# Ten products with the identity, in float32, issued as transposes of TensorE

## The chip, the cores and the metric

The kernel runs on one core of a Trainium2 chip. The metric is the device time of one execution in microseconds (us). The core's engines work side by side, each in an order of its own: TensorE (PE in the profile, with PEld for its weight loads), VectorE (DVE), ScalarE (ACT), GpSimd (POOL) and SyncE (SP), which issues most transfers. A matmul has a stationary operand, which a weight load puts into the array, and a moving operand, whose columns stream through it; the result goes to PSUM.

## The reference

One sequence of 512 tokens with 1024 features, in float32, goes through two blocks of two layers each. Cut to what matters:

```python
def first_block(x, c, ...):
    cond = silu(c)
    for l in range(2):
        sh1, sc1, g1, sh2, sc2, g2, sh3, sc3, g3 = split(cond @ w_ada[l] + b_ada[l], 9)
        x = x + 0.5 * g1 * swiglu(modulate(rms_norm(x), sh1, sc1), w_ff1_in[l], w_ff1_out[l])
        z_a, z_b, z_c = split_cols(modulate(rms_norm(x), sh2, sc2) @ w_in[l], ...)
        o = concat([rwkv7_mixer(z_a, ...), mla_mixer(z_b, ...), retention_mixer(z_c, ...)])
        x = x + g2 * (o @ w_out[l])
        x = x + 0.5 * g3 * swiglu(modulate(rms_norm(x), sh3, sc3), w_ff2_in[l], w_ff2_out[l])
    return rms_norm(x) * final_norm_g

def second_block(x, ...):
    h = x
    for l in range(2):
        p_in, dq, dk, dv, gq, gk, gv, gr, gg = split(rms_norm(h, norm1_g[l]) @ w_in[l])
        mix = concat([pool_mixer(p_in), diff_attention(dq, dk, dv), gla_mixer(gq, gk, gv, gr, gg)])
        h = h + mix @ w_out[l]
        h = h + square(relu(rms_norm(h, norm2_g[l]) @ w_mlp1[l])) @ w_mlp2[l]
    return rms_norm(h, final_norm_g)

reference = second_block(first_block(x, c, ...), ...)
```

The `rwkv7_mixer` is a linear recurrence in both directions with four heads of 64; `mla_mixer` is attention with eight heads over latent keys and values; `retention_mixer` is a decayed linear attention; `diff_attention` takes the difference of two softmax maps for each of four heads; `gla_mixer` is a gated linear attention in chunks of 64 tokens.

## The kernel before

Activations lie with the features on the 128 partitions and the 512 tokens along the free axis, in eight chunks. Wide products (`gemm`) are made of two float32r parts for each operand: three matmuls of 128x128 weights by 512 columns stand for one float32 product. The weights come by DMA as float32 and are split into the two parts by ScalarE (a cast) and VectorE (a subtraction). The program is, for each layer of the first block, a feed-forward part (`ff`), a mixer (`mixer1`) and another `ff`, then for each layer of the second block a mixer (`mixer2`) and an `mlp`. In time: the first mixers lie at about 400 to 870 and 1600 to 2100 us, the second mixers at about 2430 to 2650 and 3030 to 3250 us; the rest is wide products.

In a mixer two streams are merged. `merge` issues one stream (in `mixer1` the recurrence of `rwkv`, in `mixer2` the three mixers by turns) and fills each of its pauses with a hand-set amount of the other (the projections of the tokens, the attention, the retention). The pauses are the numbers after `yield`. The instructions so written pass through the framework's scheduler, which makes each engine's order from priorities and modelled durations and puts in the semaphores. The order on an engine is thus near the program's, but not the same everywhere.

Some steps need data turned from features on partitions to tokens on partitions, or a value of each token on all partitions. The kernel does both with a plain float32 matmul that has the data as the stationary operand and the identity (`self.ident`, 128x128) as the moving one, 128 columns at a time, four column blocks to a PSUM bank:

- `bcast` (line 503): the norm's factor of each token, one column for 128 tokens, read with a step of zero as a 128x128 stationary. It serves the norms of both blocks and the two latent norms (`mla_norms`).
- `head_bcast` (line 740): the same for factors of a head, spread to 64 columns by VectorE first.
- `rwkv_pair` (lines 985 and 996): six blocks for each pair of chunks, for each pair of heads; ScalarE copies the result out.
- `rwkv_heads` (line 1101), `mla_pair` (line 1234): outputs turned back to features on partitions.
- `diff` (lines 1651 and 1671): the difference of the softmax maps, t + 1 blocks for token tile t of a head, then the head's output.
- `gla` (lines 1709 and 1778): the keys, and the output.

An engine's calls go through a helper (`Spy.call`, line 136) that notes which tiles they name, so nearly all rows of the profile bear line 136, and the tiles tell them apart. Another product, in `mla_first`, uses `ident_r`, the identity as float32r, with a stationary of one column; the change doesn't touch it. `rms_col` makes the sum over the features with a moving operand of one column of ones.

Of the kernel before, what the change touches and what calls it, by code (L numbers as in the profile page):

```python
# [20 lines left out]
P = 128  # L21
# [26 lines left out]
# ---------------------------------------------------------------- host layout  # L48
def blocks(w, cols=P):
    """[K, N] -> [N/cols, 128, K/128*cols]: one contiguous run per partition and block."""  # L50
    k, n = w.shape
    return np.ascontiguousarray(
        w.reshape(k // P, P, n // cols, cols).transpose(2, 1, 0, 3)
    ).reshape(n // cols, P, (k // P) * cols)


def group_blocks(w, groups):
    """[K, N] -> per group of K chunks: [N/128, 128, kg*128], flattened and joined."""
    return np.concatenate([blocks(w[a * P:(a + n) * P]).ravel() for a, n in groups])
# [15 lines left out]
def make_masks():  # L75
    """constants that depend on shapes alone."""
# [23 lines left out]
def make_rows():  # L100
    """rotary frequencies and the sign of the sine, per partition, for head widths 64 and 32."""
    out = np.zeros((P, 4), np.float32)
    base = np.float32(10000.0)
    for j, d in ((0, 64), (2, 32)):
        inv = base ** (-np.arange(0, d, 2, dtype=np.float32) / np.float32(d))
        out[:, j] = np.tile(inv, P // (d // 2))
        out[:, j + 1] = np.where(np.arange(P) % d < d // 2, -1.0, 1.0)
    return out
# [11 lines left out]
# ---------------------------------------------------------------- device side  # L120
# [4 lines left out]
class Spy:  # L125
    """an engine that notes which tiles each instruction names, then issues it."""
# [21 lines left out]
class Alloc:  # L148
    """Tiles by class. A dry pass notes where each is used first and last in program order; from that each gets
    one of the class's fixed buffers, so that the buffers never force an order that the program doesn't have."""  # L150
# [17 lines left out]
    def begin(self, cls, key, n):  # L168
        """buffers (key, 0..n-1) that serve the class until `end`."""
# [5 lines left out]
    def assign(self, sizes):  # L175
        """key of the buffer for every tile, in the order of their birth."""
# [6 lines left out]
    def assign_with(self, sizes, keep):  # L183
        """the same, with `keep` buffers of a class held back from what fits into one that comes and goes."""
# [25 lines left out]
# class of buffer -> (shape, type, count); the phase's own classes follow  # L210
# [15 lines left out]
# places of the first mixer that change their use: the stages' classes; "x" lies where "h" of the phase "ff" does  # L226
# [7 lines left out]
class Build:  # L234
# [36 lines left out]
    def stage(self, i):  # L271
        """the places from the first that changes on pass over to the classes of stage i."""
# [31 lines left out]
    def lend_x(self):  # L304
        """put x into DRAM; until it is back its tiles serve as the phase's slots."""
# [49 lines left out]
    def background(self, share=None):  # L355
        """part of the work that goes on behind the first block's wide products (share None: all that is left)."""
# [23 lines left out]
    # -- weights: one block, split exactly into two float32r parts  # L380
    def weight(self, ap, n, cls="wr", sub=None):
        """(hi, lo) tiles of 512 columns each."""
# [17 lines left out]
    def gemm(self, out, w, x, ks, m=P, at=0, sl=ALL):  # L400
        """out[m, 512] = sum_k w_k^T x_k, each product of split parts; w's chunks from column `at` on."""
# [3 lines left out]
    def gemm_k(self, out, w, xk, i, n, m=P, at=0, sl=ALL):  # L405
        """chunk i of n of such a product."""
# [7 lines left out]
    def out_proj(self, load, g, update, norm=None, scale=None):  # L414
        """x[j] from its products with g, for all j. norm "sum": with the sums of squares of the next norm, the last
        j's left to `pending`; "halves": with the norm itself, the last two j by halves of the tokens, so that the first half's is there early."""
# [33 lines left out]
    # -- rsqrt of a small positive tile by DVE  # L450
# [14 lines left out]
    def sum_sq(self, acc, xc, sl=ALL):  # L465
        """acc + xc^2 (acc None: a new sum)."""
# [10 lines left out]
    def x_done(self, j, sl=ALL):  # L477
        """chunk j of x has its final value of this stage: its part of the next norm."""
        self.xsq = self.sum_sq(None if j == 0 else self.xsq, self.x[j], sl)

    def norm_half(self, i):
        """PSUM [128, 512], half i of the tokens: one over the norm of x."""
# [3 lines left out]
    def rms_col(self, chunks, dim, eps, ts=range(4)):  # L486
        """[128, 4]: 1/sqrt(mean over features of x^2 + eps) of token ts[t]*128 + partition; chunks None: of x."""
# [15 lines left out]
    def bcast(self, r, ts=range(4)):  # L503
        """PSUM [128, 512] with the token's value on every partition."""
        pr = self.aux_ps()
        for i, t in enumerate(ts):
            self.nc.tensor.matmul(pr[:, t * P:(t + 1) * P], r[:, i:i + 1].to_broadcast([P, P]), self.ident,
                                  start=True, stop=True)
# [5 lines left out]
    # -- adaptive layer norm: one section of 1024 columns  # L514
    def cond_row(self):
        """silu(c) on every partition."""
# [13 lines left out]
    def ada_dot(self, l, s, k, w):  # L530
        """chunk k of section s of 1024 columns of the modulation of layer l, less its bias."""
# [3 lines left out]
    def ada_end(self, l, s, k=0, n=KD):  # L535
        """chunks k.. of section s with their bias, and what is derived from them."""
# [10 lines left out]
    def ada_steps(self, parts):  # L547
        """the sections (layer, section) one after the other in small steps, loads ahead of them."""
# [13 lines left out]
    def modulate(self, i, k, hk, pr, sl=ALL, pool=True):  # L562
        """chunk k of h = rms_norm(x) * (1 + sc) + sh, split into hk."""
# [13 lines left out]
    def modulated(self, i, ws):  # L577
        """h of modulation i, a list of (hi, lo), and its products with the first weights, by halves of the tokens
        and as the chunks come."""
# [11 lines left out]
    def start(self):  # L591
        """the first h: its modulation is worked out chunk by chunk as the weights for it come in."""
# [26 lines left out]
    def ff(self, l, w, i, norm):  # L619
        """x += 0.5 * g * (silu(h w_gate) * (h w_up)) w_out"""  # L620
# [32 lines left out]
    # ------------------------------------------------------------ constants  # L653
    def restart(self):
        """factors of a scan over the tokens that starts anew with every chunk of 64."""
# [9 lines left out]
    def rotary_tables(self):  # L665
        """cos and signed sin of positions * inv, [128, 512] each, for head widths 64 and 32."""
# [26 lines left out]
    def derived(self, l):  # L693
        """small per-feature vectors worked out on chip for layer l of the first block."""
# [14 lines left out]
    # ------------------------------------------------------------ first mixer: RWKV-7  # L709
# [11 lines left out]
    def rwkv_z(self, l, h, ps, dv, z):  # L721
        """nine projected tiles after the centred shift (r 0-1, k 2-3, v 4-5, gate, decay and rate inputs);
        v with the chunks of each pair swapped."""
# [16 lines left out]
    def head_bcast(self, col, stride, at):  # L740
        """PSUM [128, 512] from token-major scalars of two heads, col[tok, t*stride + at + hh]."""
# [5 lines left out]
        for t in range(4):  # L747
            self.nc.tensor.matmul(pb[:, t * P:(t + 1) * P], ex[:, t * P:(t + 1) * P], self.ident,
                                  start=True, stop=True)
        return pb  # L750

    def head_sums(self, src, dst, at):
        """dst[tok, t*2 + at + hh] = sum over the head's 64 features of src [features, tok]."""
# [4 lines left out]
    def rwkv_norm(self, l, z, j):  # L758
        """one over the norm of each head's keys, token major."""
# [19 lines left out]
    def rwkv_prep(self, l, z, dv, lora, j):  # L779
        """the four scaled operands of each direction for one pair of heads.  # L780

        pr: [d, step pair, (p | r), (par, t)]; qm: [d, step pair, par, (q | m swapped by par), t]
        """
# [57 lines left out]
    def rwkv_inverse(self, os_):  # L841
        """X^T of every chunk, X = (1 + strict part)^-1: per pair of heads and direction
        [128 (par, s)][(step pair, hh), t]."""
# [29 lines left out]
        # matrix (j, m, d, (par, half)) on its own partition, m = (step pair, hh)  # L873
# [37 lines left out]
    def rwkv_blocks(self, xt, xa, u):  # L911
        """from the inverses of the 32 x 32 diagonal blocks those of the chunks, for one pair of heads."""
        nc = self.nc
        # off-diagonal 32-blocks
# [34 lines left out]
    def rwkv_pair(self, o, vs, xt, xd, ip):  # L949
        """per-chunk matrices of one pair of chunks in each direction: what the sequential steps need.  # L950
        xd: zeros, and room for the inverses of both chunks on the diagonal."""
# [31 lines left out]
        for d in range(2):  # L983
            cp = ip if d == 0 else 3 - ip
            nc.tensor.matmul(pp[:, d * P:(d + 1) * P], o["pr"][:, d, ip, 0, :], self.ident, start=True, stop=True)
# [7 lines left out]
        for d in range(2):  # L993
            for par in range(2):
                m = d * 2 + par
                nc.tensor.matmul(pt[:, m * P:(m + 1) * P], o["qm"][:, d, ip, par].rearrange("p w t -> p (w t)"),
                                 self.ident, start=True, stop=True)
# [42 lines left out]
    def rwkv_heads(self, l, z, o, xt, gate, j, out):  # L1040
        """one pair of heads: sequential steps over the chunks, head norm, bonus, gate."""
# [5 lines left out]
        # the state by turns in two halves, both heads' [key, value] on the diagonal for each direction  # L1047
# [32 lines left out]
        # head norm (the values were centred, so the mean is zero), gain, bonus, gate  # L1080
# [19 lines left out]
        for t in range(4):  # L1100
            nc.tensor.matmul(py[:, t * P:(t + 1) * P], y[:, t * P:(t + 1) * P], self.ident, start=True, stop=True)
# [33 lines left out]
    # ------------------------------------------------------------ first mixer: latent attention  # L1135
# [19 lines left out]
    def rope32(self, out, pz, n, tab):  # L1155
        """rotary over 32-wide heads on n partitions; pz in PSUM."""
# [8 lines left out]
    def mla_norms(self, l, z):  # L1165
        """the two latent norms, in place."""
# [8 lines left out]
    def mla_first(self, z, i, pk, pq, kq, qpe):  # L1175
        """operands of head i: [64 plain, 32 rotary, 1 for the maximum] x tokens, split."""
# [9 lines left out]
        # the maximum of a row of scores, taken of the rounded operands: any number near it serves  # L1186
# [800 lines left out]
```

## Time and profile before

| | |
|---|---|
| time, median of 3 runs | 3662.97 us (3648.62 to 3664.79) |
| profiled execution: span, first to last instruction | 3653.2 us |
| PE busy | 3528.1 us (97%), 17786 matmuls |
| PEld busy | 2849.3 us (78%), 17786 loads |
| DVE busy | 2103.8 us (58%) |
| ACT busy | 1436.7 us (39%) |
| POOL busy | 281.7 us (8%) |
| mean granted clock of TensorE | 0.980 |

The profiled execution's own time is known by its span alone, 3653.2 us; it lies 9.8 us below the median and inside the range of the three runs. Busy times are shares of the span; PE's records overlap one another, since matmuls are pipelined and their ends are modelled. The granted clock is 1 at 2.4 GHz and 0.5 at 1.2 GHz.

### The profile page before, as it was taken

How to read it: one execution, taken by the hardware profiler on the slowest of the kernel's cores; microseconds unless marked ns; L12 is line 12 of the kernel's file. 1: busy time of each engine (PE TensorE's matmuls, PEld its weight loads, DVE VectorE, ACT ScalarE, POOL GpSimd, SP SyncE). 2: the span in 40 equal slices, each digit the busy share in tenths (PEclk: the TensorE clock that was granted, in tenths of full speed). 3: DMA queues.
4: the chain of work that ended last, by engine and by line, in shares of the span. 5: the costliest groups of instructions: out<-in, count | busy, mean ns of one | idle time of the engine just before them, and what ended most of it. 6: DMA issues, size and time to landing. Idle time of an engine off the chain costs nothing. (4 is left out here: it accounts for less than half of the span.)

```text
span 3653.2 us, 46456 instructions
## 1 busy us (share of the span) xinstructions
PE 3528.1 (97%) x17786; PEld 2849.3 (78%) x17786; DVE 2103.8 (58%) x4153; ACT 1436.7 (39%) x2644; POOL 281.7 (8%) x344
## 2 busy tenths in 40 slices
PE   7999998999999999999899999999999999999998
PEld 5888876788888888887678888877778887778887
DVE  7954785657954534468565544366754445764444
ACT  3223544444233423245344423245443334443333
POOL 2000261100000000015210000000100000000000
PEclk9999998999999999999898999999999999999999
DMA  7833322015842222332201222221122222212222
GB/s 273 323 123 103 120 81 54 24 46 207 322 164 95 86 97 87 96 121 81 61 18 41 76 93 94 96 83 64 54 94 93 97 94 72 65 58 98 93 93 75
DMA packets 132879, 375.78 MB, mean 103 GB/s; under 512 B 37712, under 2 KB 41072, under 8 KB 132656
## 3 DMA queue, kind: packets, MB, share of 16 engines
q1 hardware_dynamic: 127808, 359.48, 29.7%
q0 software_dynamic: 3776, 12.32, 1.0%
q8 instruction: 139, 2.28, 0.3%
q10 hardware_dynamic: 1072, 1.01, 0.1%
q14 instruction: 84, 0.69, 0.1%
HBM read 362.27 MB, written 10.49 MB: 102 GB/s over the span
## 5 line engine op out<-in xcount | busy, mean ns | idle before, releaser
L136 ACT CAST wr<-raw 128x512 fp32r<-128x512 f32 (+2 forms) x1054 | 640.8, 610 | 1558.7 <-PE ps L136 1438.5
L136 DVE TENSOR_TENSOR wr<-raw,wr 128x512 fp32r<-128x512 f32 (+1 forms) x1004 | 681.4, 680 | 782.3 <-ACT wr L136 760.6
L136 PE MATMUL ps<-ff_h,wr 128*128 128x512 f32 (+1 forms) x4296 | 983.7, 390 | 10.1 <-ACT ff_h L136 7.3
L136 PEld LDWEIGHTS ps<-ff_h,wr 128*128 128x128 f32 x4296 | 794.4, 190 | 195.4 <-ACT ff_h L136 10.1
L136 PE MATMUL ps<-mlp_r,wr 128*128 128x512 f32 (+1 forms) x3120 | 716.3, 391 | 2.1 <-ACT mlp_r L136 2.1
L136 PEld LDWEIGHTS ps<-mlp_r,wr 128*128 128x128 f32 x3120 | 580.9, 188 | 135.7 <-ACT mlp_r L136 3.0
L136 PE MATMUL ps<-ff_r,wr 128*128 128x512 f32 (+1 forms) x2238 | 495.2, 382 | 0.0
L136 PEld LDWEIGHTS ps<-ff_r,wr 128*128 128x128 f32 x2238 | 404.1, 188 | 89.3
L136 PE MATMUL ps<-mix_r,wr 128*128 128x512 f32 (+1 forms) x1104 | 277.9, 402 | 1.8 <-DVE mix_s L136 1.8
L136 PE MATMUL ps<-mix_h_x,wr 128*128 128x512 f32 (+2 forms) x1104 | 261.0, 395 | 4.3 <-ACT mix_h_x L136 2.2
L136 PEld LDWEIGHTS ps<-mix_r,wr 128*128 128x128 f32 (+1 forms) x1104 | 199.4, 185 | 57.9 <-issue 5.2
L136 PEld LDWEIGHTS ps<-mix_h_x,wr 128*128 128x128 f32 (+1 forms) x1104 | 200.4, 197 | 56.0 <-issue 4.5
L136 DVE SCALAR_TENSOR_TENSOR ff_big<-ff_big,ff_big 128x1024 f32<-128x1024 f32 x144 | 176.5, 1238 | 10.3 <-DMA ff_big<-in_w_ada 9.6
L136 DVE SCALAR_TENSOR_TENSOR ff_s<-ff_s,ps 128x512 f32<-128x512 f32 x176 | 120.2, 684 | 88.1 <-PE ps L136 83.7
L136 DVE SCALAR_TENSOR_TENSOR x<-ps,hg,x 128x512 f32<-128x512 f32 (+1 forms) x102 | 73.4, 719 | 85.9 <-PE ps L136 85.7
L136 DVE TENSOR_TENSOR ps<-ps,mlp_s 128x512 f32<-128x512 f32 (+1 forms) x66 | 45.1, 683 | 105.3 <-PE ps L136 105.2
L136 ACT COPY mix_s<-ps 128x256 f32<-128x256 f32 (+7 forms) x156 | 61.6, 401 | 104.4 <-PE ps L136 75.8
L136 DVE TENSOR_TENSOR mlp_r<-mlp_s,mlp_r 128x512 fp32r<-128x512 f32 x80 | 54.6, 691 | 69.5 <-ACT mlp_r L136 69.5
L136 POOL MEMSET mix_s<- 32x256 f32 (+3 forms) x36 | 12.5, 348 | 985.6 <-DVE mix_r L136 363.9
L136 ACT ACTIVATE mix_s<-ps,m 128x512 f32<-128x512 f32 (+3 forms) x140 | 70.9, 529 | 44.0 <-PE ps L136 25.0
L136 PE MATMUL ps<-mix_s,mix_s 128*128 128x128 f32 (+7 forms) x648 | 82.7, 283 | 2.6 <-ACT mix_s L136 1.9
L136 PEld LDWEIGHTS ps<-mix_s,mix_s 128*128 128x128 f32 (+5 forms) x648 | 63.6, 169 | 16.9 <-ACT mix_s L136 7.1
(317 smaller groups left out, 3591.8 us busy)
## 6 DMA issues: line engine op xcount, KB each, us to landing
raw<-in_ff_in SPq DMA_DIRECT2D x176, 512.0 KB, 3.5
ff_big<-in_w_ada SPq DMA_DIRECT2D x144, 512.0 KB, 6.2
raw<-in_mlp SPq DMA_DIRECT2D x128, 512.0 KB, 3.5
raw<-in_ff_out SPq DMA_DIRECT2D x64, 448.0 KB, 3.3
raw<-in_ff_out SPq DMA_DIRECT2D x32, 512.0 KB, 3.6
raw<-in_out SPq DMA_DIRECT2D x32, 512.0 KB, 3.5
raw<-in_in SPq DMA_DIRECT2D x28, 512.0 KB, 3.5
raw<-in_in_a SPq DMA_DIRECT2D x18, 512.0 KB, 4.0
```

The lines of the kernel that those rows point to most:

```text
L136: self.alloc.last[self.name] = f(*a, **k)
```

## The change

Each of the ten calls keeps its output, its data and the identity, and becomes `nc.tensor.transpose`. The diff also takes out comments and docstrings (the lines stay, empty).

```diff
     def bcast(self, r, ts=range(4)):
         pr = self.aux_ps()
         for i, t in enumerate(ts):
-            self.nc.tensor.matmul(pr[:, t * P:(t + 1) * P], r[:, i:i + 1].to_broadcast([P, P]), self.ident,
-                                  start=True, stop=True)
+            self.nc.tensor.transpose(pr[:, t * P:(t + 1) * P], r[:, i:i + 1].to_broadcast([P, P]), self.ident)
...
     def head_bcast(self, col, stride, at):
         for t in range(4):
-            self.nc.tensor.matmul(pb[:, t * P:(t + 1) * P], ex[:, t * P:(t + 1) * P], self.ident,
-                                  start=True, stop=True)
+            self.nc.tensor.transpose(pb[:, t * P:(t + 1) * P], ex[:, t * P:(t + 1) * P], self.ident)
...
     def rwkv_pair(self, o, vs, xt, xd, ip):
-            nc.tensor.matmul(pp[:, d * P:(d + 1) * P], o["pr"][:, d, ip, 0, :], self.ident, start=True, stop=True)
+            nc.tensor.transpose(pp[:, d * P:(d + 1) * P], o["pr"][:, d, ip, 0, :], self.ident)
...
-                nc.tensor.matmul(pt[:, m * P:(m + 1) * P], o["qm"][:, d, ip, par].rearrange("p w t -> p (w t)"),
-                                 self.ident, start=True, stop=True)
+                nc.tensor.transpose(pt[:, m * P:(m + 1) * P], o["qm"][:, d, ip, par].rearrange("p w t -> p (w t)"), self.ident)
...
     def rwkv_heads(self, l, z, o, xt, gate, j, out):
-            nc.tensor.matmul(py[:, t * P:(t + 1) * P], y[:, t * P:(t + 1) * P], self.ident, start=True, stop=True)
+            nc.tensor.transpose(py[:, t * P:(t + 1) * P], y[:, t * P:(t + 1) * P], self.ident)
...
```

`mla_pair`, `diff` (two calls) and `gla` (two calls) change in the same way.

## Rows read from the trace of the kernel before

**Rows 1.** Page: span; busy us, share, instructions; slices in tenths, granted clock.
```profile
span 3653.2 us, 46456 instructions
PE 3528.1 (97%) x17786; PEld 2849.3 (78%) x17786; DVE 2103.8 (58%) x4153; ACT 1436.7 (39%) x2644; POOL 281.7 (8%) x344
...
PE   7999998999999999999899999999999999999998
...
PEclk9999998999999999999898999999999999999999
```

**Rows 2.** Chain of waits, shares, 1888 to 1965 us and 2560 to 2650 us.
```profile
by line: PE ps L136 83.7%; DVE m L136 4.9%; DVE mix_s L136 2.6%; DVE mix_r_x L136 2.5%; DVE x L136 2.1%; ACT wr L136 1.6%; issue 1.5%; DVE wr L136 1.2%; ACT mix_r_x L136 0.6%; DVE mr L136 0.1%
...
by line: PE ps L136 86.6%; DVE mix_s L136 5.0%; ACT mix_r L136 3.4%; ACT mix_s L136 2.8%; DVE m L136 1.0%; DVE mix_r L136 0.8%; issue 0.6%; DVE ps L136 0.1%
```

**Rows 3.** Identity's tile by stretches: from:to, length, busy us (records), clock, DMA.
```profile
0.00:3653.00 3653.00, 123.16 (x784) 107.14 (x784) 0.30 (x1) 0.98 0.31 103
400.00:870.00 470.00, 35.01 (x224) 30.31 (x224) 0.00 (x0) 0.94 0.22 68
1600.00:2100.00 500.00, 36.31 (x224) 31.61 (x224) 0.00 (x0) 0.93 0.20 61
2430.00:2650.00 220.00, 21.94 (x152) 19.39 (x152) 0.00 (x0) 1.00 0.19 61
3030.00:3250.00 220.00, 22.27 (x144) 19.61 (x144) 0.00 (x0) 0.98 0.18 59
```

**Rows 4.** Tiles ident, ones, ident_r: records, duration ns min/median/max, starts.
```profile
L136 PEld LDWEIGHTS ps<-ident,mix_rw x192: 186/192/192, 593.5 to 1912.8; 128*128 128x128 f32 x192
L136 PE MATMUL ps<-ident,mix_rw x192: 275/275/377, 593.5 to 1912.9; 128*128 128x128 f32 x192
...
L136 PE MATMUL ps<-ones,sq x128: 164/250/371, 17.2 to 3642.0; 128*128 128x1 f32 x128
...
L136 PE MATMUL ps<-ident_r,mr x64: 218/223/348, 700.5 to 2005.2; 128*1 128x128 f32 x64
```

**Rows 5.** Timeline of PE and its loads at 594, 2445, 1911 us: start, us, what.
```profile
594.37 0.97 PEld L136 LDWEIGHTS ps<-ident,mix_rw 128*128 128x128 f32 x8
...
2445.04 1.10 PEld L136 LDWEIGHTS ps<-ones,sq 128*128 128x128 f32 x8
...
2445.28 0.95 PE L136 MATMUL ps<-ones,sq 128*128 128x1 f32 x8
...
1911.18 0.40 PE L136 MATMUL ps<-ident_r,mr 128*1 128x128 f32 x4
```

**Rows 6.** Timeline of all engines, 2451.7 to 2453.5 us: a broadcast of a norm.
```profile
2451.53 0.40 PE L136 MATMUL ps<-wr,mix_r 128*128 128x512 f32 x1
...
2452.05 0.97 PEld L136 LDWEIGHTS ps<-ident,m 128*128 128x128 f32 x8 [0.56 <-DVE m L136]
2452.05 1.16 PE L136 MATMUL ps<-ident,m 128*128 128x128 f32 x8
...
2453.25 0.75 DVE L136 SCALAR_TENSOR_TENSOR x<-x,vec,ps 128x512 f32<-128x512 f32 x1 [1.25 <-PE ps L136]
```

**Rows 7.** Stretches, all work: busy of PE, PEld, DVE, ACT, POOL; clock; DMA.
```profile
590.00:770.00 180.00, 174.46 (x1393) 137.91 (x1389) 123.42 (x318) 87.40 (x191) 24.10 (x46) 1.00 0.10 31
770.00:810.00 40.00, 38.46 (x199) 33.50 (x198) 15.20 (x30) 16.68 (x30) 0.00 (x0) 0.79 0.04 14
1791.00:1960.00 169.00, 164.77 (x1303) 130.38 (x1303) 113.37 (x300) 76.93 (x171) 21.91 (x42) 0.96 0.08 22
2430.00:2650.00 220.00, 213.53 (x1074) 163.57 (x1073) 161.68 (x424) 108.37 (x231) 10.49 (x15) 1.00 0.19 61
3037.00:3250.00 213.00, 207.07 (x1024) 158.54 (x1025) 145.33 (x390) 101.36 (x218) 9.85 (x13) 0.98 0.18 58
```

More of the change, by code (lines that the diff above doesn't have):

```diff
@@ L1233, in mla_pair @@
             sl = slice(t * P, (t + 1) * P)
-            self.nc.tensor.matmul(pt[:, sl], ot[:, sl], self.ident, start=True, stop=True)
+            self.nc.tensor.transpose(pt[:, sl], ot[:, sl], self.ident)
         return self.split(pt)
@@ L1650, in diff @@
                 for c in range(t + 1):
-                    nc.tensor.matmul(pt[:, c * P:(c + 1) * P], ps[0][:, c * P:(c + 1) * P], self.ident,
-                                     start=True, stop=True)
+                    nc.tensor.transpose(pt[:, c * P:(c + 1) * P], ps[0][:, c * P:(c + 1) * P], self.ident)
                 at = self.slot()
@@ L1670, in diff @@
             for t in range(4):
-                nc.tensor.matmul(pf[:, t * P:(t + 1) * P], o[:, t * P:(t + 1) * P], self.ident, start=True, stop=True)
+                nc.tensor.transpose(pf[:, t * P:(t + 1) * P], o[:, t * P:(t + 1) * P], self.ident)
             t = self.slot()
@@ L1708, in gla @@
         for t in range(4):
-            nc.tensor.matmul(pk[:, t * P:(t + 1) * P], ke[:, t * P:(t + 1) * P], self.ident, start=True, stop=True)
+            nc.tensor.transpose(pk[:, t * P:(t + 1) * P], ke[:, t * P:(t + 1) * P], self.ident)
         kt = self.slot()
@@ L1777, in gla @@
             for t in range(4):
-                nc.tensor.matmul(pf[:, t * P:(t + 1) * P],
-                                 os_[t // 2][:, (t % 2) * 256 + j * P:(t % 2) * 256 + (j + 1) * P], self.ident,
-                                 start=True, stop=True)
+                nc.tensor.transpose(pf[:, t * P:(t + 1) * P],
+                                 os_[t // 2][:, (t % 2) * 256 + j * P:(t % 2) * 256 + (j + 1) * P], self.ident)
             nc.vector.scalar_tensor_tensor(th, pf, self.v(f"gla_norm_g{l}", j), th, ALU.mult, ALU.mult)
```

## The prediction

> **What bounds the kernel now.** I read the page's header and its slices first [rows 1]. TensorE (PE) is busy for 3528.1 us of a span of 3653.2 us, 97%, and its digit is 9 in nearly all of the 40 slices; VectorE reaches 58%. The reader is to see there that no stage leaves PE idle for long, and that PEclk drops to 8 in three slices, all in the first mixers. A busy PE is not yet a full PE, because matmuls are pipelined, so I read next the chain of waits inside the two kinds of mixer, where the change is made [rows 2]: PE's own work makes up 83.7% of it in a piece of the first mixer and 86.6% in a piece of the second. The rest are hand-overs through VectorE and ScalarE. So a nanosecond taken from PE in a mixer is mostly, and not wholly, a nanosecond of the span.
>
> Then I asked for the identity's tile alone, by stretches [rows 3] and with the durations [rows 4]. The matmuls that name it are 784 records, with a 128x128 stationary and 128 columns in float32. The program issues 392 of them: 64 column blocks in `bcast`, 48 in `head_bcast` (12 calls of four), 96 in `rwkv_pair` (16 calls of six), 16 and 32 in `rwkv_heads` and `mla_pair`, 112 in `diff` (14 for each of four heads and two layers) and 24 in `gla`. So each float32 matmul is two pairs of a weight load and a matmul. By stage: 224 records lie in 400 to 870 us and 224 in 1600 to 2100 us (the first mixers and the norms at their edges), 152 and 144 in the second mixers, 40 elsewhere.
>
> **The change part by part.** Ten call sites change, all in one way: the same output, the same stationary data and the same 128 columns of identity, as a transpose. Nothing moves in the program text, and no buffer, DMA or wait is added. The comments and docstrings that go are no instructions and cost nothing.
>
> What one costs now. In a run of eight such records [rows 5] the weight loads take 0.97 us from the first start to the last end, and one lasts 0.192 us [rows 4]: (0.97 - 0.192) / 7 = 0.111 us a step. One product with the identity is two steps, 0.223 us, and the 392 are 87 us of PE's time when nothing waits.
>
> What sets the step? In the same group, eight float32 matmuls with a stationary of 128 columns and ONE moving column go at (0.95 - 0.250) / 7 = 0.100 us from PE's row and (1.10 - 0.192) / 7 = 0.130 from the loads' (the first load waits a little for its matmul), so 0.11 us in the mean, the same as with 128 columns. The load of 128 float32 weights alone explains the step. A transpose moves bits and can't be a sum of a high and a low part, so I expect one record pair where there were two, still with its load: 0.111 us. Saved: 0.111 us each, 392 x 0.1115 = 43.7 us. By stage that is 224 x 0.1115 = 25.0 us in the two first-mixer stretches together, 148 x 0.1115 = 16.5 us in the second mixers, 2.2 us elsewhere.
>
> The trace shows no transpose, so here are both ends. Cheapest: a step that the weight load doesn't bind. The nearest row is the product of `ident_r`, with one stationary column and 128 moving columns in one pass: (0.40 - 0.223) / 3 = 0.059 us. Saved 0.164 us each, 64 us. Dearest: transposes that don't overlap one another or the matmuls around them. Then each would cost the full latency of a record, 0.275 us [rows 4], that is 0.052 us more than two steps now: 20 us lost. I take 0.111 us, because the row with one moving column has the same stationary and data type, and a transpose has to load it as well.
>
> What of it is on the path. The first mixers' chain is 84% PE, so I keep 0.80 of 25.0 us = 20.0 us, less than the share because a step in `rwkv_heads` hands its result to ScalarE and back. The second mixers keep 0.87 of 16.5 us = 14.4 us. Elsewhere the transposes stand alone on the path between a norm's root and the first use of the broadcast. One such group shows the pattern [rows 6]: PE idles 0.56 us for VectorE's `m`, runs the eight records, and VectorE idles 1.25 us until the last. Here all of the 2.2 us stays. Together 36.6 us. What hides the rest (about 7 us): PE arrives earlier at an operand that a chain on VectorE or ScalarE delivers as late as before, so that operand is what is late next.
>
> The clock. In the four stretches with most transposes the granted clock is 1.00, 0.96, 1.00 and 0.98 [rows 7], at 2.4 GHz nearly always; yet between them, at 770 to 810 us, it is 0.79, part of the time at the 1.2 GHz level, where PE did little dense work. One step in place of two leaves PE less to do in the same stretch, so the clock could fall oftener. A fall of the mean clock from 1.00 to c over T us costs at most (1 - c) x T: the slow part is 2(1 - c)T long and half of it is lost. The four stretches are 782 us. I allow a fall by 0.004, 3 us.
>
> The order. The instructions aren't run as written: `proj2`'s products (wr, mix_r) run ahead of the broadcast on the identity [rows 6], which stands before them in the text. The order is the framework's plan, made from modelled durations, and it may be made anew when 392 instructions become another kind. I know no sign for this; it is worth some 8 us either way, the size of the waits in the mixers that a new order could add or close (7 us hidden above).
>
> Sum: 36.6 - 3 = 33.6 us off the profiled execution, 3653.2 to 3619.6 us of span. The median of the runs shown is 3662.97 us, 9.8 us above that span, and the runs span 3648.62 to 3664.79, so the span fits among them; with the same distance the time is 3629 us.
>
> One place of the Trainium skill speaks of the price, "TensorE: Matmul & The Clock Gate", section Terms: on trn2 loads and matmuls have a transpose mode that is four times as fast for float32. By it one product falls from 0.223 to 0.056 us, close to the row of `ident_r`, and the sum would be 65 us before what is hidden; no run so far shows it, and the row with one moving column speaks against it for the load.
>
> **The rivals.**
> (B) The weight load in transpose mode is quick too, and a step is 0.059 us. For it: nothing binds but 128 columns. Against it: the row with one moving column. It gives 64 us x 36.6 / 43.7 = 54 us less 4 us for the clock: 3613 us.
> (C) The mixers don't keep it: their end is set by the chains through VectorE and ScalarE, and PE only waits more. For it: PE's records overlap, so its 97% hides small waits, and the steps of `rwkv_heads` and the softmax of `diff` go to and fro between three engines. Against it: the shares of the chain [rows 2]. If a quarter of the mixers' 41.5 us stays, that is 10 us + 2 us: 3651 us, within 0.5%.
> (D) Slower: the clock. Transposes don't keep PE's clock up, and in the stretches rich in them it falls as at 770 to 810 us. For it: the clock is already below 1.00 in two of the four [rows 7]. The same page of the Trainium skill, Part 4 (PE-mode transpose), states that a transpose doesn't count as busy time for the clock; no row of the kernel before can show it. Against it: the transposes themselves are 0.111 us x 372 = 41 us in 782 us, dense products lie between them, and the load-bound steps of today do little dense work either, yet the clock holds. It decides from a fall of the mean clock by 36.6 / 782 = 0.047: there all of the gain is gone. At 0.79 for 40% of the 782 us the cost is 0.21 x 313 = 66 us, so 29 us slower: 3692 us.
> (E) It doesn't do what it says: the transpose is issued as two pairs as well, or its step is 0.22 us. Nothing in the trace speaks for it but that float32 has always two records here. It gives 3663 us.
>
> **How the numbers follow.** The forecast has 0.46, B 0.20, C 0.16, D 0.08, E 0.06; 0.04 is left for a new order that costs more than the gain (slower). The predicted time is the forecast's, 3629 us; its own range, with the order's 8 us and 5 us for what is kept, is 3616 to 3642. The range for 8 in 10 reaches to the full 64 us kept, 3663 - 64 = 3599, less some for a better order, so 3596, and on the other side to E, 3663, and 3 us of spread between runs: 3666. Only D and the bad order lie outside, and the tails of B. Half a percent, 18 us, is about what a measurement of this kernel can tell from no change, since three runs of it differ by 16 us. Faster by more than that are the forecast, B and a little of C, together 0.68; within it most of C, and E, 0.21; slower 0.11.
>
> **What would show it.** In the profile after: 392 records on `ident` and as many loads in place of 784; a run of four with a step of 0.11 us between the loads (0.06 would be B, 0.22 E, 0.275 the dear end); PE's busy time in the identity's rows down by about half; PEclk in the four stretches within 0.01 of now (a fall by 0.05 is D); the second mixers shorter by about 7 us each and the first by about 10 us each (if PE's waits for VectorE and ScalarE grow instead, it is C). The prediction is wrong if a transpose costs other than one load, or if the stretches move by more than their identity rows do.

## The result and the profile after

The changed kernel takes 3601.44 us in the median of four runs (3599.74 to 3605.91), where the kernel before takes 3658.47 us in four runs beside it: a ratio of 0.985, with a 95% interval of 0.983 to 0.987. Measured a second time, on the same chip as some of the experiments below, it is 3607.73 us and a ratio of 0.9877 (0.9855 to 0.990). The mean of its eight runs is 3604.8 us. The forecast was 3629 us with a range of 3596 to 3666: the direction and the range held, and the gain was larger than the 34 us forecast.

The page of the changed kernel answers to [rows 1].

```profile
span 3604.1 us, 45671 instructions
PE 3477.7 (96%) x17394; PEld 2797.2 (78%) x17394; DVE 2098.5 (58%) x4153; ACT 1435.7 (40%) x2644; POOL 278.6 (8%) x344
PE   6999998999999999999899999999999999999998
PEclk9999998999999999999899999999999999999999
```

392 matmuls and as many loads are gone; VectorE, ScalarE and GpSimd carry out as many instructions as before. The span is 49.1 us shorter, of which PE's busy time gives 50.4 us. What is not busy on PE (span less busy time) is 125.1 us before and 126.4 us after: PE is still nearly always at work.

The identity's tile, by the whole span and for the group of RWKV, answers to [rows 3] and [rows 4] (the first row has from and to, length, then busy time and records of PE, PEld and ScalarE, the clock and the DMA).

```profile
0.00:3604.00 3604.00, 72.15 (x392) 48.40 (x392) 0.30 (x1) 0.98 0.30 104
L136 PEld LDWEIGHTS ps<-ident,mix_rw x96: 138/142/230, 592.7 to 1890.7; 128*128 128x128 f32 x96
L136 PE MATMUL ps<-ident,mix_rw x96: 272/273/472, 592.7 to 1890.8; 128*128 128x128 f32 x96
```

A matmul record is as long as it was (273 ns, 275 before), since what one record shows is mostly latency. Half as many records, and a load of 0.142 us in place of 0.192, are what changed. That is why a mean duration says little on a pipelined engine, and the step from one start to the next has to be found.

The broadcast of a norm before the second mixer answers to [rows 6] (timeline of all engines: start, length, what; in brackets the idle time before it and who ended it).

```profile
2422.72 0.41 PEld L136 LDWEIGHTS ps<-ident,m 128*128 128x128 f32 x4 [0.57 <-DVE m L136]
2422.72 0.65 PE L136 MATMUL ps<-ident,m 128*128 128x128 f32 x4
...
2423.41 1.41 DVE L136 SCALAR_TENSOR_TENSOR x<-x,vec,ps 128x512 f32<-128x512 f32 x2 [0.74 <-PE ps L136]
```

PE waits for `m` as long as before (0.57 us, 0.56 then), and VectorE's wait for the last block falls from 1.25 to 0.74 us: 0.51 us for four transposes in place of four products. The step in this run of four is (0.41 - 0.142) / 3 = 0.09 us from the loads' row and (0.65 - 0.273) / 3 = 0.126 us from PE's, 0.11 us in the mean.

The chain of waits inside the mixers, 1870 to 1945 us and 2530 to 2620 us, answers to [rows 2].

```profile
by line: PE ps L136 84.5%; DVE mix_s L136 4.1%; DVE mix_r_x L136 2.5%; DVE m L136 2.4%; DVE x L136 2.2%; DVE wr L136 1.8%; ACT wr L136 1.7%; ACT mix_r_x L136 0.8%; issue 0.6%
...
by line: PE ps L136 82.3%; DVE mix_s L136 7.1%; ACT mix_r L136 3.4%; ACT mix_s L136 2.8%; DVE m L136 2.2%; DVE mix_r L136 1.4%; issue 0.8%; DVE ps L136 0.2%
```

In the second mixer PE's share of the chain falls from 86.6% to 82.3% and that of VectorE's `mix_s` rises from 5.0% to 7.1%; in the first it stays (83.7%, 84.5%).

To see where the 49.1 us are, I cut both executions at the first matmul of each stage. The four mixers stand first for the kernel before, then for the changed one (from:to, length, PE's busy time and matmuls, granted clock, DMA).

```profile
409.60:854.70 445.10, 415.31 (x2827) 0.94 0.19 56
1612.30:2062.70 450.40, 422.02 (x2826) 0.93 0.19 55
2437.20:2676.70 239.50, 232.99 (x1156) 1.00 0.19 63
3037.80:3278.30 240.50, 234.32 (x1141) 0.99 0.19 63
```

```profile
409.70:841.00 431.30, 400.13 (x2718) 0.95 0.20 58
1598.00:2034.90 436.90, 407.09 (x2718) 0.93 0.19 58
2407.80:2638.70 230.90, 225.32 (x1080) 1.00 0.19 66
2999.30:3230.10 230.80, 225.63 (x1068) 0.99 0.19 65
```

The first mixers are shorter by 13.8 and 13.5 us, the second by 8.6 and 9.7, and all other stages together by 3.5 us. The fall is in PE's busy time in each of the four. For the first mixers this is one execution of each kernel only, and one and the same program can differ by 11 us there (e3 and e6 below), so their 13.8 and 13.5 us are not the change's alone.

### The profile page after: what moved, and what is told of

Read it like the earlier page. It is cut to its first block, busy times and chain, and to the rows that moved or that the text cites. A ratio compares the mean times of both kernels' runs of the same rounds, so it can differ in the third digit from the quotient of the medians.

```text
span 3604.1 us, 45671 instructions
## 1 busy us (share of the span) xinstructions
PE 3477.7 (96%) x17394; PEld 2797.2 (78%) x17394; DVE 2098.5 (58%) x4153; ACT 1435.7 (40%) x2644; POOL 278.6 (8%) x344
## 5 line engine op out<-in xcount | busy, mean ns | idle before, releaser
L136 POOL MEMSET mix_s<- 32x256 f32 (+3 forms) x36 | 12.5, 348 | 973.8 <-DVE mix_r L136 362.5
```

What stands on the lines that cost most here:

```text
L136: self.alloc.last[self.name] = f(*a, **k)
```

## The experiments

Three causes could move the time: the step of a transpose, PE's waits, and the granted clock; and the planner's new order could work through the last two. The first experiment measures the step alone, the next ones part the step from the order, the last ones part the change itself.

**e1: what sets the step.** TensorE alone; the whole computation of the reference is left out. Stretches of one kind of matmul follow one another, with 90 dense float32r products between them.

```
for i in range(160): mm(bank[:, c:c+128], data, ident)          # L59: 2 records each
for i in range(320): tr(bank[:, c:c+128], data, ident)          # L63
for i in range(320): tr(bank[:64, c:c+128], data[:, :64], ident)      # L67: 64 stationary columns
for i in range(320): tr(bank[:, c:c+64], data[:64], ident[:64, :64])  # L71: 64 moving columns
for i in range(320): mm(bank[:, c:c+1], data, one)              # L75: one moving column
```

> Leaves out the whole computation: TensorE alone works, in stretches of one kind each, with 90 dense float32r products of 512 columns (about 21 us) between them, so that the clock starts high in each. Stretches: 160 float32 products with the identity; 320 transposes of 128x128; 320 transposes with a stationary of 64 columns; 320 transposes of 64 partitions, that is 64 moving columns; 320 float32 products with one moving column; 60 products with the identity, each followed by a dense product; 60 transposes, each followed by a dense product. Theory (the load of the weights sets a transpose's step): 0.109 us for the 128x128 transposes, about 0.055 with 64 stationary columns, still 0.109 with 64 moving columns; 0.223 us for a float32 product with the identity, the same with one moving column. Rival (the moving columns set the step): 64 stationary columns leave 0.109, 64 moving columns give about 0.055. For the clock: if transposes don't keep it up, the granted clock falls to 0.5 within the 320 transposes (35 us) and not in the 160 products with the identity (36 us); theory of the prediction: it holds in both, or falls in both alike. Alternating with a dense product: the transpose saves 0.114 us of a pair, as alone; if a change of mode costs, less, down to nothing.

The timeline of PE (start, length of the stretch, records), then the same instructions' loads (records, busy us, mean ns):

```profile
26.89 35.89 PE L59 MATMUL ps<-ident,data 128*128 128x128 f32 x320
62.54 20.66 PE L48 MATMUL ps<-wide 128*128 128x512 f32 x90
83.04 35.09 PE L63 MATMUL ps<-ident,data 128*128 128x128 f32 x320
...
138.42 35.09 PE L67 MATMUL ps<-ident,data 128*64 128x128 f32 x320
...
193.89 20.47 PE L71 MATMUL ps<-ident,data 64*128 64x64 f32 x320
```

```profile
L59 PEld LDWEIGHTS ps<-ident,data 128*128 128x128 f32 x320 | 35.9, 192 | 0.1
L63 PEld LDWEIGHTS ps<-ident,data 128*128 128x128 f32 x320 | 35.0, 140 | 0.1
L67 PEld LDWEIGHTS ps<-ident,data 128*64 128x64 f32 x320 | 34.9, 111 | 0.2
...
L71 PEld LDWEIGHTS ps<-ident,data 64*128 64x128 f32 x320 | 20.3, 140 | 0.4 <-issue 0.4
```

160 products take as long as 320 transposes. Less the latency of the last record, a product's record steps by (35.89 - 0.275) / 319 = 0.112 us, two of them make 0.223 us; a transpose steps by (35.09 - 0.273) / 319 = 0.109 us. The saving is 0.114 us, for 392 of them 44.7 us. With half the stationary columns the step stays at 0.109 us; with 64 moving columns on 64 rows it is (20.47 - 0.223) / 319 = 0.063 us, though each load still has 128 columns. The load's record follows its own columns (140 ns for 128, 111 ns for 64, 140 ns again for 128 on 64 rows), and the step does not follow the load's record. So the columns that move past set a float32 transpose's step, and not the load: the theory fell and its rival held. No stretch halves the rows alone, so their part in the 0.063 us is not parted from that of the columns.

The granted clock of the transposes' stretch and of the stretch with one moving column:

```profile
83.00:118.00 35.00, 35.00 (x322) 1.00 0.00 1
232.00:366.00 134.00, 134.00 (x640) 0.52 0.00 1
```

Through 35 us of nothing but transposes, behind 90 dense products, the clock stays at 1.00, 2.4 GHz. Through 134 us of products with one moving column, where PE does little but load weights, it is 0.52, nearly all at 1.2 GHz, and a record steps by 0.21 us. The Trainium skill, "TensorE: Matmul & The Clock Gate", Part 4 (PE-mode transpose), states that the full clock doesn't engage for a transpose, which doesn't count as PE-busy in the same way. The trace doesn't agree as far as holding the clock goes: by that rule it should have fallen in the stretch of transposes as it did in the one-column stretch. Whether transposes alone would raise a clock that is low, no run here shows.

**e2 and e3: the order without the steps, the steps without the order.** In e2 the products of the kernel before run in the order that the changed kernel's instructions have on each engine; in e3 transposes run in the order of the kernel before. The edges that fix the order carry no wait of their own. The traces show that the orders were met: of some 17100 weight loads, about 235 stand elsewhere in the changed kernel than in the kernel before, while e2 has every engine's instructions, as far as the names of their tiles tell, in the order of the changed kernel and e3 in that of the kernel before.

```
+ def ordered(nc, tc, names):          # names: the other kernel's order
+     for n in names: add_manual_dep(instr[n], last_on_its_engine, NoSync)
```

> The matmuls with the identity, as before the change, in the order of instructions that the changed kernel has on every engine. Theory (the gain is TensorE's step time, and the new order is worth nothing): the time of before, 3658 us within 6 us. Rival (a part of the 57 us comes from the new order, as the step time alone gives 45 us): 3646 us, 12 us under the kernel before.

> The transposes, in the order of instructions that the kernel before has on every engine. Theory (step time alone, all kept): 3658 less 45 to 57 us, 3601 to 3613 us. Rival (the order gives some 12 us): 3613 us or above. Second rival (in the old order the waits for VectorE and ScalarE eat a part, as the prediction had it): about 3622 us.

e2 takes 3657.28 us, ratio 1.0012 (0.9993 to 1.0031): the new order alone is worth nothing that can be measured. e3 takes 3618.02 us, ratio 0.9895 (0.9874 to 0.9916): the steps alone are worth 38 us by the medians.

**e5 and e6: the changed kernel and e3 once more, on one chip.** No edit; asked is whether the 17 us between them are real.

> The changed kernel itself, unaltered, on the same chip as the next run. Theory 1 (the new order is worth something once the steps are short): ratio to the kernel before 0.983 to 0.987, some 12 to 17 us below the transposes in the old order (e6). Rival (the order is worth nothing and the gap between the two earlier sets of runs is chance): within 5 us of e6, both near 3610.

> The transposes in the order of the kernel before on every engine, a second time. Theory 1: 3618 us again, ratio 0.9895, 12 to 17 us above e5. Rival (chance): as e5, near 3610.

e5 is 3607.73 us (0.9855 to 0.990), e6 3612.02 us, ratio 0.9894 (0.987 to 0.9918): 4 us apart, with intervals that overlap and both near 3610 us, so by its medians this set goes to the rival. Over both sets the changed kernel has a mean of 3604.8 us (8 runs) and the transposes in the old order 3616.4 us (11 runs), with a scatter of about 4 and 8 us a run, so the order is worth some 12 us beside the transposes, give or take 6. Neither 17 nor nothing.

The pages of e2, e3, e6 and e5, in this order, show 6 us of it (span, then busy times).

```profile
span 3652.5 us, 46455 instructions
PE 3532.9 (97%) x17786; PEld 2845.8 (78%) x17786; DVE 2097.2 (57%) x4153; ACT 1438.2 (39%) x2644; POOL 279.4 (8%) x344
```

```profile
span 3615.9 us, 45672 instructions
PE 3483.6 (96%) x17394; PEld 2795.5 (77%) x17394; DVE 2101.5 (58%) x4153; ACT 1436.3 (40%) x2644; POOL 281.8 (8%) x344
```

```profile
span 3613.4 us, 45672 instructions
PE 3480.7 (96%) x17394; PEld 2793.2 (77%) x17394; DVE 2101.3 (58%) x4153; ACT 1436.1 (40%) x2644; POOL 282.0 (8%) x344
```

```profile
span 3601.8 us, 45671 instructions
PE 3474.8 (96%) x17394; PEld 2788.1 (77%) x17394; DVE 2096.9 (58%) x4153; ACT 1436.1 (40%) x2644; POOL 279.0 (8%) x344
```

Span less PE's busy time is PE's idle time. In the old order it is 125.1 us with products and 132.3 and 132.7 us with transposes; in the new order 119.6 with products and 126.4 and 127.0 with transposes. So in these executions transposes add 7 us of waits in either order, and the new order takes 6 us away with either kind. PE's waits say which the order moves (us, times, longest; two rows of each view, those between left out; the kernel before, e2, e3, the changed kernel):

```profile
PE ps L136 <- DVE mix_s L136: 25.2, 14, 6.4
PE ps L136 <- ACT mix_r_x L136: 5.6, 6, 1.0
```

```profile
PE ps L136 <- DVE mix_s L136: 19.3, 13, 4.8
PE ps L136 <- ACT mix_r_x L136: 4.2, 6, 1.0
```

```profile
PE ps L136 <- DVE mix_s L136: 25.4, 18, 6.6
PE ps L136 <- ACT mix_r_x L136: 7.0, 6, 1.6
```

```profile
PE ps L136 <- DVE mix_s L136: 22.7, 16, 6.3
PE ps L136 <- ACT mix_r_x L136: 4.5, 6, 1.0
```

They are the mixers' hand-overs through VectorE and ScalarE. Together they are 30.8, 23.5, 32.4 and 27.2 us: the new order takes 7.3 us off them with products and 5.2 us with transposes. Of the 7 us that the transposes add, they hold only 1.6 us in the old order and 3.7 us in the new; the rest is spread over waits of which none grew by more than 1.7 us.

The clock moves the time as well, since the same program gets another share of low clock in each execution. Here are the first mixers of e3, then of e6, one program run twice:

```profile
409.40:840.60 431.20, 398.20 (x2719) 0.95 0.20 58
1596.70:2039.00 442.30, 413.00 (x2718) 0.92 0.20 57
```

```profile
409.20:851.80 442.60, 413.34 (x2718) 0.92 0.19 57
1607.80:2039.40 431.60, 398.11 (x2718) 0.95 0.20 58
```

The two mixers have changed places: 11 us go with a mean clock of 0.92 in place of 0.95, on the same 2718 matmuls. Summed over the trace's clock records, the time at 1.2 GHz is 147.8 us before, 155.4 in e2, 148.0 and 144.6 in e3 and e6, 143.6 and 130.9 in the two profiled executions of the changed kernel. Two executions of each are few, but every execution on record has its mean granted clock beside its time. Through the 105 executions of the kernel before (in the two later sets), of the changed kernel and of e2 to e8 go lines of one slope: 3.15 us for each 0.001 of mean clock, with a scatter of 2.1 us about them. The last column is an estimate from that slope.

| | executions | mean time, us | mean clock | time at a clock of 0.980, us |
|---|---|---|---|---|
| kernel before | 42 | 3656.1 | 0.9793 | 3653.9 |
| e2 (products, new order) | 12 | 3660.4 | 0.9774 | 3652.3 |
| e3 and e6 (transposes, old order) | 11 | 3616.4 | 0.9810 | 3619.6 |
| changed kernel | 8 | 3604.8 | 0.9815 | 3609.5 |

At one clock the order is worth 10 us beside the transposes, give or take 2 (11 us in the first set, 9 in the second), and 1.6 us beside the products, give or take 1.4. So the clock has less than 2 of the 12 us. Of the 10, 6 are PE's waits; where the rest lies is not shown. In e2 a clock lower by 0.0019 costs 6 us, yet even at one clock its 6 us less of waits show as 1.6. One rival is left untested: e2, e3 and e6 have the edges that force the order, the other two kernels don't, and no run forces a kernel's own order on it. If the edges cost some 4 us, both differences are 6 us, the size of the waits. Beside transposes the clock is the same in both orders within its error of 0.001, and 0.002 higher than in the kernel before; why it is higher, and why e2's is lower, stays open.

**e4: every transpose issued twice.** Each of the ten call sites has its line a second time.

```
  self.nc.tensor.transpose(pt[:, sl], ot[:, sl], self.ident)
+ self.nc.tensor.transpose(pt[:, sl], ot[:, sl], self.ident)
```

> Every transpose is issued twice, one after the other, with the same output. Theory (each step of TensorE in a mixer counts fully): 392 x 0.109 = 43 us more than the changed kernel, about 3644 us, still some 10 us under the kernel before, whose product takes 0.223 us against 0.218. Rival (steps are partly hidden behind waits, share kept about 0.85): 36 us more, 3638 us, or less.

It takes 3644.2 us, ratio 0.9963 (0.9948 to 0.9979), 12.5 us below before and some 40 us above the changed kernel. The median is the theory's time. But at a clock of 0.980 it is 3642.4 us by the same estimate, 33 us above the changed kernel, where 392 more steps of 0.109 us are 42.7 us, and this goes to the rival: in the kernel, too, a transpose costs most of its step, and not all of it. The planner gave e4 nearly the order of the kernel before (some 80 loads stand elsewhere), so e3 and e6 are the fairer comparison, and there the second transposes cost 23 us. The page shows a part of why that is less.

```profile
span 3654.4 us, 46456 instructions
PE 3530.4 (97%) x17786; PEld 2847.7 (78%) x17786; DVE 2102.5 (58%) x4153; ACT 1436.4 (39%) x2644; POOL 281.3 (8%) x344
```

PE's idle time is 124.0 us, as with products (125.1) and not as with one transpose (132.3 and 132.7): the second transposes fill some 8 us that PE waits for otherwise.

**e7 and e8: the change in parts.** Transposes only in `diff` and `gla` (e7), only in `head_bcast`, `rwkv_pair`, `rwkv_heads` and `mla_pair` (e8); all other sites keep `matmul(..., self.ident, start=True, stop=True)`.

> Transposes only in the two second mixers (148 of 392), everything else as matmuls with the identity; the planner sets its own order. Theory 1 (steps times kept share, parts add up): 148 x 0.114 = 16.9 us of steps, of which 0.87 are kept: 14.7 us below the kernel before, near 3642. Rival (the second mixers gain from the order too, as the two -8.5 and -9.7 us of the changed kernel say): 18 us below, near 3638. Rival (the order is worth some 8 us either way by chance): anywhere from 3634 to 3650.

> Transposes only in the first mixers' own functions (192 of 392), everything else as matmuls with the identity; the planner sets its own order. Theory 1 (steps times kept share): 192 x 0.114 = 21.9 us of steps, of which 0.80 are kept: 17.5 us below the kernel before, near 3639. Rival (as the -13.8 and -13.5 us of the two first mixers in the changed kernel say): 27 us below, near 3630. Rival (order by chance): 3630 to 3647.

e7 takes 3641.74 us, ratio 0.9966 (0.9952 to 0.9979), 12.5 us less; e8 3636.47 us, ratio 0.9955 (0.9935 to 0.9976), 17.8 us less. The expectation of e7 has a slip: those two functions hold 136 transposes, and 148 counts the broadcasts in the second mixers as well. By its reckoning 136 x 0.114 x 0.87 = 13.5 us were due. Both parts are near the first theory, and the rivals that took more from the stages of the changed kernel missed by 6 and 9 us; the wide ranges of the rivals by chance hold both times and are not excluded. The 64 of `bcast` are left, 7.3 us of steps, which no run has alone; 12.5 + 17.8 + 7.3 = 37.6 us, less than the 46 to 57 us of the whole. The clock closes this gap: at 0.980 the two parts lie 14.7 and 20.9 us below the kernel before (3639.2 and 3633.0 us), with `bcast` 42.9 us, and the whole is 44.4 us. The planner's order is nearly that of the kernel before in e7 (some 30 loads stand elsewhere) and nearly that of the changed kernel in e8 (some 70), so what the order gives should lie for the most part in e8's share.

**e9: would another type step faster?** e1 with one more stretch, transposes of float32r data; the computation is left out here too.

```
+ for i in range(320): tr(bank[:, c:c+128].bitcast(F32R), wide, idr)   # L81
```

> TensorE alone, as e1, with one more stretch: 320 transposes of 128x128 float32r data with a float32r identity; the whole computation of the reference is left out. Theory (the moving columns set the step, and float32 columns run at half the pace of float32r ones): about half of the float32 transpose's 0.109 us, 0.05 to 0.06 us a transpose. Rival (a transpose moves its columns at one pace whatever the type): 0.109 us again. The other stretches as in e1: 0.223 us a product, 0.109 us a transpose, 0.109 with 64 stationary columns, 0.064 with 64 moving ones.

```profile
392.28 27.26 PE L81 MATMUL ps<-idr,wide 128*128 128x128 f32 x320
```

(27.26 - 0.249) / 319 = 0.085 us, between the two: neither theory holds. The loads' records are 140 ns here too, so what sets this step is not shown. At all 392 places it would be worth at most 392 x 0.0245 = 9.6 us more. But this data had been rounded to float32r by ScalarE ahead of the stretch, while the kernel transposes full float32 values. In the kernel it wasn't tried. The stretches that e9 shares with e1 take the same time again: 35.89, 35.09, 35.09 and 20.47 us.

## Why the prediction was right, and where its size was off

**The count and the step.** 392 records, as forecast. The step in a stream is 0.109 us where 0.111 was forecast, and the saving 44.7 us where 43.7 was. The size was right and the reason wrong, so the size was luck: the load was said to set a transpose's step because a product with one moving column had the same one [rows 5]. For a float32 product the rows fit that; a transpose's load is quicker (0.140 us long, 0.192 for a product), and then its 128 moving columns bind. By its own sign, that a transpose costs other than one load, this step of the prediction failed. The row of `ident_r` [rows 4], on which rival B rested, differs in two things, one stationary column and float32r data. A float32r transpose with 128 stationary columns steps by 0.085 us in e9 and not by 0.059 us, so the type alone does not make that row's pace, and one stationary column is not a transpose's load.

**What of it is kept.** The forecast kept 36.6 of 43.7 us, a share of 0.84. In the old order 38 of 44.7 us came through by the medians, 0.85, but with a clock higher by 0.0017; at one clock it is 34.4 us, 0.77. Of the 10 us lost, 7 stand in the trace as more of PE's waits; the rest is not placed, and a part may be the forced edges. This is rival C's mechanism, at about the size that the forecast gave it and not at C's. In the planner's own order the whole change keeps 44.4 of 44.7 us at one clock, as the order gives back what the waits take.

**The order.** "Some 8 us either way" with no sign was entered at nothing. It was a gain of 6 us in PE's waits, shown by all four pairings of order and kind of instruction; in time it is 10 us beside transposes at one clock, as far as forcing an order costs nothing. This is the first of two mis-sized terms.

**The clock.** It was entered as 3 us lost. The time at 1.2 GHz fell by 4.2 us in one profiled execution and by 16.9 us in the other; counted at half, as at that level PE's work takes twice as long, this is a gain of 2 and 8 us. Over all executions the mean clock rose from 0.9793 to 0.9815, which is 7 us by the slope above. This is the second mis-sized term, wrong in sign; no run shows what raised the clock. The expected clock in the four stretches held only in the second mixers: 590 to 770 us went from 1.00 to 0.97, while 770 to 810 us, at 0.79 in [rows 7], is at 1.00 now. The low stretches wander, so one stretch of one execution says little; the sum, and better the mean over executions, says something.

**The sum.** Spans fell by 49.1 and 51.4 us. PE's busy time, with the low-clock time counted at half, fell by (3528.1 - 73.9) - (3477.7 - 71.8) = 48.3 us in the one and by 44.9 us in the other, against 44.7 us of steps; waits added 1.3 and 1.9 us (7 from the transposes less 6 from the order), the clock gave 2.1 and 8.5 us. The two sums are 49.1 and 51.5 us; that they meet the spans is arithmetic, since a span is PE's busy and idle time, and the test is the busy time against the steps. Over all executions the mean gain is 3656.1 - 3604.8 = 51.3 us, 44.4 us at one clock and 6.9 us by the clock. The forecast had 36.6 and -3 us for these two: it lacked 8 us of steps and order together, and 10 us of clock. Its time started besides from a median of 3663 us, 7 us above the mean of the kernel before. The stages moved by about what their identity rows make (109 and 108 steps of 0.114 us in the first mixers, 76 and 73 in the second, so 12.4, 12.3, 8.7 and 8.3 us against 13.8, 13.5, 8.6 and 9.7).

**The rivals.** B (3613 us) lay nearer to the time than the forecast, but for another cause: a step of 0.06 us is shown, among transposes, only with 64 moving columns on 64 rows. Its page's figure, the Trainium skill's "TensorE: Matmul & The Clock Gate", Terms, that transpose mode is four times as fast for float32, is not what e1 shows: 0.223 to 0.109 us in a stream is a factor of 2.05. C holds as a small part, D fell with e1's clock of 1.00 and with the changed kernel's mean clock, which is higher than before, E with the 392 records.

## What to carry to other kernels

Take the price of a TensorE instruction from the step between starts in a stream of the same kind: the records' 273 and 275 ns would have promised nothing. If a row is to stand in for an operation that the trace lacks, check that type, stationary and moving columns all agree; one that agrees in one of them gave the right number here by chance. Where a tensor engine's clock wanders, one execution of a kernel differs from the next by 11 us in a single stage, so read a stage's change together with its clock, compare times at one clock where each execution's clock is known (here the scatter falls from 4 to 10 us a run to 2), and part the order from the instructions before a cause is named. If an order is forced for that, force a kernel's own order too, so that the cost of forcing is known.

## What was not expected of the hardware

A transpose of 128x128 float32 steps by 0.109 us with 128 or 64 stationary columns, by 0.063 us with 64 moving columns on 64 rows, and by 0.085 us in float32r. A stream of transposes alone, behind dense products, held the clock at 1.00; float32 products with one moving column let it fall to 0.52, and then a record took 0.21 us in place of the 0.11 us in [rows 5]. Beside a dense product that alternates with it, the transpose keeps its advantage: in e1 a pair steps by 0.453 us with a product and by 0.343 us with a transpose, 0.11 us less, where 0.114 was expected.
